# Long convolutions by quarters of the channels, two quarters one stage apart, and z kept unscaled

## The chip, the cores and the metric

One core of one Trainium2 chip runs the whole block in one launch. The metric is device microseconds per execution. Before the change three runs took 1247.49, 1248.54 and 1249.72 us (median 1248.54). The profiled execution that all rows come from took 1252.21 us.

## The reference, cut to what matters

A hybrid layer on x of 2048 positions by 1024 channels, all in float32:

```python
h = rms_norm(x, pre_g);  p = h @ w_in                       # 1024 -> 3072
hy = short_conv(p[:, :1536], conv_w, conv_b)                # 3 taps
v, gates = hy[:, :512], (hy[:, 512:1024], hy[:, 1024:])
k_f = two_sided_spectrum(hyena_filters(...))                # an MLP over positions
y = v
for o in range(2):
    y = gates[o] * fft_conv(y, k_f[:, o], hyena_d[o])       # two long convolutions
y_h = rms_norm(y * silu(z_h), norm_h_g)
y_p = rms_norm(multiscale_pool(u_p) * silu(z_p), norm_p_g)
out = x + rms_norm(concat(y_h, y_p) @ w_out, post_g)
```

## The kernel before, in words

The kernel is written in a tile framework. A planner takes the instructions in the order of the program as priorities, and gives each engine a fixed order in which an instruction may pass earlier ones that are not ready; each engine and each DMA queue then works in that order. Tiles of one tag share `bufs` buffers, and a new tile waits for the last use of the tile whose buffer it takes. PSUM has eight banks.

**Projection (0 to 600 us).** TensorE multiplies x by the columns of `w_in`, with every float32 operand split into two float32r parts (high and low) and three matmuls per product (`mm`, lines 313 to 320, five PSUM banks; `nm`, lines 541 to 543). x enters unnormalised; the rows' factors (`rb`, from `stat_x`) are multiplied in when a block leaves PSUM. In the first round, for each of four position blocks, `mm_tr` makes the pool branch's z and u. A z block is held in PSUM (`zps`) until the next round, when `stat_x` has its factors and `silu_evac` (line 325) reads it. The u blocks stay in PSUM too, up to `pool_means`.

**Long convolutions (600 to 1118 us).** Each is a transform of length 2048 written as matmuls in two steps, for 256 channels at a time: half `hf`, order `o`. The units run in the order (0,0), (1,0), (0,1), (1,1) as (order, half):

- `pre_k` makes the filter: `gen` (line 631, weights `HT`, 256 moving columns) makes filter values, DVE multiplies by the decay, GpSimd and DVE make sums and differences `sd`, `s1k` (line 644) does the first transform step, and the result goes to `BK`. `trans` then transposes 32x32 blocks on DVE.
- `pre_s` loads v and does the first transform step (`s`, three float32r matmuls in `mm3`) into `BS`.
- `gloop` is the loop over 16 groups: `kern` makes the filter's spectrum (`pk`), ACT copies it, two DMAs swap its halves (`kk`); `mult` makes the signal's spectrum (`px`) and the complex product with DVE, GpSimd and ACT; `back` is the inverse step (`pc`), which DVE copies into `BS`.
- `post0` finishes the inverse (`dd`, `py`), multiplies by the gate and does the first step of the next order into `BS`. `post1` does the last step of order 1, times the second gate, and stores `y_d`.
- `fill` computes the pool branch's half of the output product (`fp`, lines 769 to 771): 32 blocks that depend on nothing here. They are written between the stages.

There is one `BK` and one `BS` buffer of 32 KB per partition each. The banks are: `k` 2, `x` 2, `pk` 2, `c` 1, `f` 1; `s` shares `x`, and `py` uses `c` and `pk`.

**Output (1118 us to the end).** For four position blocks `split_y` makes the operand from `y_d` (first half of the channels) and from two `post1` of the second half; `out_mm` makes `po`; `finish` adds the stored `fp` part, normalises, adds x and stores.

All loads and stores of the convolutions are issued on SP's queue.

Of the kernel before, what the change touches and what calls it, by code (L numbers as in the profile page):

```python
# [37 lines left out]
def _tables():  # L38
# [53 lines left out]
    dt = dt.reshape(128, 8, 2, 2, 2, 256).transpose(4, 1, 0, 2, 3, 5)  # L92
# [13 lines left out]
def _layouts(inp):  # L106
# [33 lines left out]
    o["fwo"] = a["filt_w_out"][0].reshape(64, 2, 2, 2, 256)  # L140
# [8 lines left out]
def build(tc, I, out, debug=None):  # L149
# [442 lines left out]
    BK = kp.tile([P, R, 256, 2], F32, tag="BK", name="BK")  # L592
    BS = kp.tile([P, R, 256, 2], F32, name="BS")
# [8 lines left out]
    def trans(B, cbs=range(8)):  # L602
        for cb in cbs:
            ap = B[:, :, cb * 32:cb * 32 + 32].rearrange("p a c i -> p c a i")
            V.transpose(out=ap, in_=ap)  # L605

    def pre_k(o, hf):
        u = f"{o}{hf}"
        kw = wp.tile([P, 1024], F32, tag="wraw", name=f"kw{u}", bufs=1)
        wr, hd = kw[:, 0:512], kw[0:1, 512:768]  # L610
        for h in range(2):
            Q.dma_start(out=wr[64 * h:64 * h + 64].rearrange("p (a c) -> p a c", a=2), in_=I["fwo"][:, o, :, hf])
        Q.dma_start(out=hd, in_=I["hd"][o:o + 1, hf * 256:hf * 256 + 256])
        wh = hp.tile([P, 512], F32R, tag="kwh", name=f"kwh{u}", bufs=1)
        wl = hp.tile([P, 512], F32R, tag="kwl", name=f"kwl{u}", bufs=1)
        S.copy(out=wh, in_=wr)
        V.tensor_tensor(out=wl, in0=wr, in1=wh, op=ALU.subtract)
        sds = {}

        def gen(m):  # L620
            dc = kp.tile([P, 2, 2, 256], F32, tag="dec", name=f"dec{u}_{m}", bufs=2)
            (S if u == "00" and m < 2 else Q).dma_start(out=dc, in_=I["t_dec"][hf, m])
            ab = abp.tile([P, 2, 2, 256], F32, tag="ab", name=f"ab{u}_{m}", bufs=2)
            for i in range(2):
                n2 = 2 * m + i
                ps = psB.tile([P, 2, 256], F32, tag="k", name=f"gen{u}_{n2}", bufs=2)
                for dr in range(2):
                    c0 = n2 if dr == 0 else 16 - n2
                    lh = HT[:, c0 % R, c0 // R:c0 // R + 128]
                    for k_, wt in enumerate((wh, wl)):  # L630
                        T.matmul(ps[:, dr], lh, wt[:, dr * 256:dr * 256 + 256], start=(k_ == 0), stop=(k_ == 1))
                V.tensor_tensor(out=ab[:, i], in0=ps, in1=dc[:, i], op=ALU.mult)  # L632
                if n2 == 0:
                    G.tensor_tensor(out=ab[0:1, 0, 0], in0=ab[0:1, 0, 0], in1=hd, op=ALU.add)
            sd = wp.tile([P, 2, 2, 256], F32, tag="wh", name=f"sd{u}_{m}", bufs=3)
            G.tensor_tensor(out=sd[:, 0], in0=ab[:, :, 0], in1=ab[:, :, 1], op=ALU.add)  # L636
            V.tensor_tensor(out=sd[:, 1], in0=ab[:, :, 0], in1=ab[:, :, 1], op=ALU.subtract)
            sds[m] = sd

        def s1k(m):  # L640
            sd = sds.pop(m)
            for ri in range(2):
                ps = psB.tile([P, 2, 256], F32, tag="k", name=f"s1k{u}_{m}_{ri}", bufs=2)
                T.matmul(ps, f1[:, ri], sd[:, ri], start=True, stop=True)  # L644
                (V.tensor_copy if ri else S.copy)(out=BK[:, ri * 8 + m].rearrange("p c i -> p i c"), in_=ps)

        for m in range(9):
            if m < 8:
                gen(m)
# [12 lines left out]
    def pre_s(o, hf, cs=(0, 1)):
        for c in cs:
            for m in range(8):
                ut = abp.tile([P, 2, 2, P], F32R, tag="ut", name=f"ut{o}{hf}_{m}_{c}", bufs=3)
                Q.dma_start(out=ut.bitcast(F32), in_=v_d[hf, m, c])
                s1(f"{o}{hf}", m, c, ut)
            trans(BS, range(4 * c, 4 * c + 4))

    def gloop(o, hf, after=None):  # L670
        u = f"{o}{hf}"

        gs = [2 * (m // 2) + 16 * (m % 2) for m in range(16)]
# [13 lines left out]
        def mult(m):  # L687
            kk = kks.pop(m)
            px = psB.tile([P, 2, 256], F32, tag="x", name=f"px{u}_{m}", bufs=2)
            for i in range(2):  # L690
                T.matmul(px[:, i], gf[:, gs[m] + i], BS[:, gs[m] // 2, :, i], start=True, stop=True)  # L691
            xs = fp.tile([P, 2, 256], F32, tag="xs", name=f"xs{u}_{m}", bufs=2)
            S.mul(out=xs[0:64], in_=px[64:128], mul=-1.0)
            S.copy(out=xs[64:128], in_=px[0:64])  # L694
            yt = fp.tile([P, 2, 256], F32, tag="yt", name=f"yt{u}_{m}", bufs=3)
# [22 lines left out]
        back(15)  # L718
        trans(BS)

    def post0(hf):
        for c in range(2):
            cs = slice(128 * c, 128 * c + 128)
            uts = {}
            for m in range(9):
                if m < 8:
                    if m % 2 == 0:
                        gt = fp.tile([P, 4, P], F32, tag="gt", name=f"gt0{hf}_{m}_{c}", bufs=2)
                        Q.dma_start(out=gt, in_=g0_d[hf][:, 2 * m:2 * m + 4, cs])
                    dd = wp.tile([P, 2, 2, 2, P], F32R, tag="wl", name=f"dd{hf}_{m}_{c}", bufs=3)  # L730
                    src = BS.rearrange("p (r a) c i -> p r a c i", r=2)[:, :, m, cs].rearrange("p r c i -> p r i c")
                    S.copy(out=dd[:, 0], in_=src)
                    (V if m % 2 else G).tensor_tensor(out=dd[:, 1], in0=src, in1=dd[:, 0], op=ALU.subtract)
                    ps = psB.tile([P, 2, P], F32, tag=("c", "pk")[m % 2], name=f"py0{hf}_{m}_{c}", bufs=1 + m % 2)
                    for ri in range(2):
                        mm3(ps, 2 + ri, dd[:, 0, ri], dd[:, 1, ri], ri == 0, ri == 1)
                    g_ = gt[:, 2 * (m % 2):2 * (m % 2) + 2]
                    V.tensor_tensor(out=g_, in0=ps, in1=g_, op=ALU.mult)
                    ut = abp.tile([P, 2, 2, P], F32R, tag="ut", name=f"ut1{hf}_{m}_{c}", bufs=3)
                    S.copy(out=ut[:, 0], in_=g_)  # L740
                    V.tensor_tensor(out=ut[:, 1], in0=g_, in1=ut[:, 0], op=ALU.subtract)
# [205 lines left out]
```

## Time and profile before

| | us |
|---|---|
| median of three runs | 1248.54 |
| profiled execution / its span | 1252.21 / 1250.4 |
| PE busy | 1156.9 (93%) |
| DVE / POOL / ACT busy | 859.8 / 469.5 / 440.6 |
| projection, convolutions, output | 0 to 600, 600 to 1118, 1118 to 1250.4 |

A row of the view by line gives the line, the engine, the operation, the written and the read tiles, the shapes, the count, busy time and mean duration in ns, then the engine's idle time just before and what ended it. PE is a matmul, PEld the load of its weights. A float32 matmul appears as two recorded matmuls, a float32r matmul as one; both show as f32.

### The profile page before, as it was taken

Reading aid. Unit: us, or ns where it says so; the run is one execution under the profiler, and the core shown is the slowest. Engines: PE = TensorE matmul, PEld = TensorE weight load, DVE = VectorE, ACT = ScalarE, POOL = GpSimd, SP = SyncE. Lnnn points to the kernel's source line nnn. Section 1 sums busy time; section 2 is a strip of 40 time slices with the busy share of each in tenths; the row PEclk is TensorE's granted clock in tenths of the full one; section 3 lists DMA queues with packets and bytes.
Section 4 is the critical chain, followed back from the end, with each engine's and each line's share of the span. In section 5 each row is a group of like instructions: output and inputs, shape, how many; then the busy total and the mean of one; then the engine's idle time right before and its main releaser. Section 6 shows DMA issues by size and latency. Waiting matters only on the chain.

```text
span 1250.4 us, 16966 instructions
## 1 busy us (share of the span) xinstructions
PE 1156.9 (93%) x6040; PEld 945.9 (76%) x6040; DVE 859.8 (69%) x1419; ACT 440.6 (35%) x724; POOL 469.5 (38%) x416
## 2 busy tenths in 40 slices
PE   7799999999999999989888999999999999988894
PEld 5688888877887999889656686678677767777683
DVE  6965357446365576586688888685858974769887
ACT  7612111112111110210147563653375625833321
POOL 2302020413554296585515432430233421444444
PEclk9999999999999999999999999999999999999997
DMA  7204130421432353522786336546673367564764
GB/s 259 87 31 131 43 101 23 129 96 43 138 124 65 115 150 93 150 79 95 251 251 192 97 111 209 149 104 219 215 199 93 121 202 241 118 187 149 247 214 147
DMA packets 110628, 177.25 MB, mean 142 GB/s; under 512 B 11076, under 2 KB 58960, under 8 KB 109264
## 3 DMA queue, kind: packets, MB, share of 16 engines
q1 hardware_dynamic: 108720, 173.20, 45.0%
q10 hardware_dynamic: 1648, 2.44, 0.7%
q8 instruction: 48, 0.79, 0.3%
q0 software_dynamic: 176, 0.53, 0.1%
q14 instruction: 36, 0.29, 0.1%
HBM read 113.75 MB, written 44.56 MB: 127 GB/s over the span
## 4 chain that ended last, share of the span: by engine, by line
PE 54%; DVE 18%; DMA 10%; issue 8%; ACT 5%; POOL 5%; SPq 1%; DVEq 0%; POOLq 0%; ACTq 0%
PE mm L317 7%; PE mm L319 7%; PE mm L318 7%; PE pc L705 3%; PE pk L679 3%; PE s1k L644 3%; PE nm L541 3%; PE nm L542 3%; PE nm L543 3%; PE px L691 3%; DMA a2p<-a 2%; PE fp L769 2%; PE fp L770 2%; PE fp L771 2%; DVE o L899 2%
## 5 line engine op out<-in xcount | busy, mean ns | idle before, releaser
L541 PE MATMUL nm<-wh,XH 128*128 128x256 f32 x512 | 144.8, 283 | 7.5 <-DVE a L548 6.7
L542 PE MATMUL nm<-wl,XH 128*128 128x256 f32 x512 | 144.8, 283 | 0.0
L543 PE MATMUL nm<-wh,XL 128*128 128x256 f32 x512 | 144.7, 283 | 0.0
L697 POOL TENSOR_TENSOR xs<-xs,kk 128x512 f32<-128x512 f32 x64 | 84.8, 1329 | 119.1 <-ACT xs L694 79.7
L548 DVE SCALAR_TENSOR_TENSOR a<-nm,r_nat,wc 128x256 f32<-128x256 f32 x192 | 81.5, 475 | 51.4 <-DMA a0p<-a 13.6
L541 PEld LDWEIGHTS nm<-wh,XH 128*128 128x128 f32 x512 | 97.5, 190 | 8.6 <-DVE a L548 7.8
L317 PE MATMUL mm<-XH,wh 128*128 128x512 f32 x256 | 103.0, 402 | 0.0
L319 PE MATMUL mm<-XH,wl 128*128 128x512 f32 x256 | 102.2, 399 | 0.0
L318 PE MATMUL mm<-XL,wh 128*128 128x512 f32 x256 | 101.5, 396 | 0.0
L636 POOL TENSOR_TENSOR sd<-ab 128x512 f32<-128x512 f32 x32 | 53.0, 1655 | 118.8 <-DVE ab L632 118.4
L543 PEld LDWEIGHTS nm<-wh,XL 128*128 128x128 f32 x512 | 96.9, 189 | 0.0
L542 PEld LDWEIGHTS nm<-wl,XH 128*128 128x128 f32 x512 | 96.7, 189 | 0.0
L705 PE MATMUL pc<-yt,gi 128*128 128x256 f32 x256 | 69.1, 392 | 14.7 <-DVE BS L706 7.8
L605 DVE STREAM_TRANSPOSE BS<-BS 128x1024 f32<-128x1024 f32 x64 | 73.5, 1209 | 7.4 <-ACT BS L660 7.4
L696 DVE TENSOR_TENSOR yt<-px,kk 128x512 f32<-128x512 f32 x64 | 44.0, 687 | 44.5 <-ACT xs L694 24.5
L691 PE MATMUL px<-BS,gf 128*128 128x256 f32 x256 | 69.9, 394 | 2.8 <-DVE BS L605 1.8
L679 PE MATMUL pk<-BK,gf 128*128 128x256 f32 x256 | 71.9, 393 | 0.2
L705 PEld LDWEIGHTS pc<-yt,gi 128*128 128x128 f32 x256 | 44.5, 189 | 34.7 <-DVE BS L706 15.8
L660 ACT COPY BS<-s 128x512 f32<-128x512 f32 x64 | 39.8, 628 | 79.8 <-PE s L589 76.0
L644 PE MATMUL s1k<-sd,f 128*128 128x512 f32 x128 | 63.5, 605 | 4.7 <-POOL sd L636 3.9
L698 DVE TENSOR_TENSOR yt<-yt,xs 128x512 f32<-128x512 f32 x64 | 54.0, 844 | 14.0 <-POOL xs L697 11.9
L317 PE MATMUL mm<-XH,whz 128*128 128x512 f32 x128 | 54.1, 423 | 9.7 <-ACT XH L284 6.1
(208 smaller groups left out, 3089.4 us busy)
## 6 DMA issues: line engine op xcount, KB each, us to landing
kk<-kk SPq DMA_DIRECT2D x128, 128.0 KB
fy<-yp_d SPq DMA_DIRECT2D x32, 512.0 KB
dec<-t_dec SPq DMA_DIRECT2D x30, 512.0 KB
wr<-w SPq DMA_DIRECT2D x16, 512.0 KB
ut<-v_d SPq DMA_DIRECT2D x32, 256.0 KB
gt<-g_d SPq DMA_DIRECT2D x32, 256.0 KB
op_d<-fo SPq DMA_DIRECT2D x32, 256.0 KB
o<-op_d SPq DMA_DIRECT2D x32, 256.0 KB
```

Of the source, the lines that this page charges most:

```text
L317: T.matmul(ps, wh, XH[lb][:, d], start=(d == 0), stop=False)
L318: T.matmul(ps, wh, XL[lb][:, d], start=False, stop=False)
L319: T.matmul(ps, wl, XH[lb][:, d], start=False, stop=(d == NT - 1))
L541: T.matmul(ps, xh[:, d, ls], wh, start=(d == 0), stop=False)
L542: T.matmul(ps, xh[:, d, ls], wl, start=False, stop=False)
L543: T.matmul(ps, xl[:, d, ls], wh, start=False, stop=(d == NT - 1))
L548: V.scalar_tensor_tensor(out=a[s], in0=ps, scalar=r_nat[:, l2:l2 + 1], in1=wc[:, s], op0=ALU.mult, op1=ALU.mult)
L644: T.matmul(ps, f1[:, ri], sd[:, ri], start=True, stop=True)
L679: T.matmul(pk[:, i], gf[:, gs[m] + i], BK[:, gs[m] // 2, :, i], start=True, stop=True)
L691: T.matmul(px[:, i], gf[:, gs[m] + i], BS[:, gs[m] // 2, :, i], start=True, stop=True)
L697: G.tensor_tensor(out=xs, in0=xs, in1=kk[:, 1], op=ALU.mult)
L705: ins = T.matmul(pc[:, i], gi[:, gs[m] + i], yt[:, i], start=True, stop=True)
```

## The change: what it does

The convolutions run in quarters of 128 channels. `BK` and `BS` become two buffers of 16 KB each. `pre_k`, `pre_s`, `gloop`, `post0` and `post1` no longer emit their work; each returns a list of steps. `run` merges the lists: the main list (mostly a loop) in order, the steps of each side list at even places up to 0.88 of the main one. The loop has 8 groups of four 128-column matmuls instead of 16 groups of two 256-column ones. `pc` is copied by ACT instead of DVE; all of `dd`'s subtracts are on GpSimd. The banks are `k` 2, `s` 2 (for `s` and `py`), `pk` 1, `x` 1, `c` 1, `f` 1. The result of the third quarter is stored and loaded again too, so that the output stage holds one `py1` per block. `xt` has two buffers instead of three. In the first round the first three z blocks are copied out of PSUM unscaled, and scaled later from SBUF.

```diff
+    def raw_evac(ci, lb, ps):
+        z = st.tile([P, 512], F32, tag="z", name=f"z{ci}_{lb}", bufs=3)
+        S.copy(out=z, in_=ps)
+        return z
...
         zn = mm_tr(0, 1, lb)
+        if lb < 3:
+            zn = raw_evac(0, lb, zn)
...
-            zs.append(silu_evac(0, lb - 1, zps))
+            zs.append(silu_evac(0, lb - 1, zps, zps))
...
+    def run(main, *sides, upto=0.88):
+        ev = [(i / len(main), 0, i, f) for i, f in enumerate(main)]
+        for k, sd in enumerate(sides):
+            ev += [((j + 0.5) / len(sd) * upto, k + 1, j, f) for j, f in enumerate(sd)]
+        for e in sorted(ev, key=lambda e: e[:3]):
+            e[3]()
...
-            ab = abp.tile([P, 2, 2, 256], F32, tag="ab", name=f"ab{u}_{m}", bufs=2)
-            for i in range(2):
-                n2 = 2 * m + i
-                ps = psB.tile([P, 2, 256], F32, tag="k", name=f"gen{u}_{n2}", bufs=2)
...
-                        T.matmul(ps[:, dr], lh, wt[:, dr * 256:dr * 256 + 256], start=(k_ == 0), stop=(k_ == 1))
+            ab = abp.tile([P, 4, 2, P], F32, tag="ab", name=f"ab{u}_{j}", bufs=2)
+            for h in range(2):
+                ps = psB.tile([P, 2, 2, P], F32, tag="k", name=f"gen{u}_{j}_{h}", bufs=2)
+                for i in range(2):
...
+                            T.matmul(ps[:, i, dr], lh, wt[:, dr * P:dr * P + P], start=(k_ == 0), stop=(k_ == 1))
...
-            pk = psB.tile([P, 2, 256], F32, tag="pk", name=f"pk{u}_{m}", bufs=2)
-            for i in range(2):
-                T.matmul(pk[:, i], gf[:, gs[m] + i], BK[:, gs[m] // 2, :, i], start=True, stop=True)
-            kk = wp.tile([P, 2, 2, 256], F32, tag="wl", name=f"kk{u}_{m}", bufs=3)
+            pk = psB.tile([P, 4, P], F32, tag="pk", name=f"pk{u}_{m}", bufs=1)
+            for k in range(4):
+                T.matmul(pk[:, k], gf[:, 4 * m + k], BK[o, q][:, 2 * m + k // 2, :, k % 2], start=True, stop=True)
+            kk = wp.tile([P, 2, 4, P], F32, tag="kk", name=f"kk{u}_{m}", bufs=2)
...
-            V.tensor_copy(out=BS[:, gs[m] // 2].rearrange("p c i -> p i c"), in_=pc)
+            S.copy(out=BS[q][:, 2 * m:2 * m + 2].rearrange("p a c i -> p a i c"), in_=pc)
...
-        kern(0)
-        kern(1)
-        for m in range(16):
-            mult(m)
-            if m + 2 < 16:
-                kern(m + 2)
+        r = [lambda: kern(0)]
+        for m in range(8):
+            if m + 1 < 8:
+                r.append(lambda m=m: kern(m + 1))
+            r.append(lambda m=m: mult(m))
             if m:
-                back(m - 1)
...
-    pre_k(*units[0])
...
-    gloop(0, 0)
-    post0(0)
-    pre_k(1, 0)
-    fill(range(0, 8))
-    gloop(1, 0)
...
+    run(pre_k(0, 0) + [tables], pre_s(0), fills(0, 5), upto=1.0)
+    run(gloop(0, 0), seq(pre_k(0, 1), pre_s(1)), fills(5, 9))
+    run(gloop(0, 1), post0(0), pre_k(1, 0), fills(9, 12))
+    run(gloop(1, 0), post0(1), pre_k(1, 1), fills(12, 15))
+    run(gloop(1, 1), seq(post1(0), pre_s(2)), pre_k(0, 2), fills(15, 18))
+    run(gloop(0, 2), seq(post1(1), pre_s(3)), pre_k(0, 3), fills(18, 21))
+    run(gloop(0, 3), post0(2), pre_k(1, 2), fills(21, 24))
+    run(gloop(1, 2), post0(3), pre_k(1, 3), fills(24, 28))
...
+    run(gloop(1, 3, held), post1(2),
+        [lambda ct=ct: split_wo(op, ct, 0, O0[:, 0, ct], O0[:, 1, ct], "wor") for ct in range(4)])
+    for cb in range(4):
+        trans(BS[3], cb)
```

`held` issues the last four fills behind the last `pc`, as before.

## Rows read from the trace of the kernel before

**Rows 1.** The page's first section: busy us (share of the span) xinstructions.
```profile
PE 1156.9 (93%) x6040; PEld 945.9 (76%) x6040; DVE 859.8 (69%) x1419; ACT 440.6 (35%) x724; POOL 469.5 (38%) x416
```

**Rows 2.** Busy time by stretch: length, then each engine, clock, DMA share, GB/s.
```profile
600.00:1118.00 518.00, 474.23 (x2302) 359.52 (x2300) 392.46 (x529) 274.07 (x469) 177.44 (x128) 0.99 0.58 172
675.00:700.00 25.00, 24.30 (x106) 19.45 (x107) 20.66 (x31) 21.05 (x37) 11.99 (x9) 1.00 0.56 135
716.00:752.00 36.00, 34.30 (x229) 29.54 (x228) 31.70 (x54) 25.18 (x50) 12.51 (x9) 1.00 0.38 120
800.00:825.00 25.00, 25.00 (x109) 19.84 (x109) 17.43 (x27) 19.77 (x35) 10.99 (x9) 0.99 0.48 111
1055.00:1080.00 25.00, 23.24 (x101) 17.90 (x100) 17.85 (x27) 21.49 (x37) 9.55 (x8) 1.00 0.66 176
1118.00:1250.40 132.40, 105.90 (x506) 87.56 (x504) 109.38 (x276) 37.96 (x86) 57.02 (x30) 0.91 0.57 192
0.00:100.00 100.00, 86.30 (x378) 68.72 (x379) 70.81 (x139) 50.06 (x62) 23.25 (x23) 0.95 0.38 129
```

**Rows 3.** Waits of PE from 600 to 1118: us in total, times, longest.
```profile
PE pc L705 <- DVE BS L706: 7.8, 9, 2.2
PE pc L705 <- DVE yt L698: 6.6, 5, 1.9
PE s L587 <- DMA ut<-v_d: 4.3, 6, 1.4
PE fp L769 <- ACT fo L793: 3.9, 6, 0.8
PE s1k L644 <- POOL sd L636: 3.9, 5, 1.5
PE fp L769 <- DMA fy<-yp_d: 3.1, 2, 2.2
```

**Rows 4.** Waits of PE from 0 to 100 us.
```profile
PE mm L317 <- DVE r4t L195: 3.6, 1, 3.6
```

**Rows 5.** Waits of PE from 1118 us to the end.
```profile
PE py L755 <- DVE rp L186: 5.4, 1, 5.4
PE py L755 <- DVE gt L757: 2.3, 1, 2.3
```

**Rows 6.** PE in order of time: start, length, instruction, count.
```profile
29.94 1.95 PE L260 MATMUL wp<-pw,wu 128*128 128x128 f32 x16
31.72 0.95 PE L300 MATMUL ssx<-one,xsq 128*128 128x1 f32 x8
...
629.54 0.28 PE L631 MATMUL gen<-kwl,HT 128*128 128x256 f32 x1
629.65 0.28 PE L631 MATMUL gen<-kwh,HT 128*128 128x256 f32 x1
...
676.27 1.07 PE L691 MATMUL px<-BS,gf 128*128 128x256 f32 x4
...
843.76 0.40 PE L755 MATMUL py<-f,BS 128*128 128x128 f32 x2
844.00 0.40 PE L756 MATMUL py<-f,BS 128*128 128x128 f32 x2
```

**Rows 7.** The view by line, shapes apart (columns as above).
```profile
L631 PE MATMUL gen<-kwh,HT 128*128 128x256 f32 x128 | 37.8, 318 | 3.0 <-DVE a L548 1.5 <-DVE BK L645 1.5
L706 DVE COPY BS<-pc 128x512 f32<-128x512 f32 x64 | 43.8, 684 | 4.6 <-PE pc L705 4.5
L660 ACT COPY BS<-s 128x512 f32<-128x512 f32 x64 | 39.8, 628 | 79.8 <-PE s L589 76.0 <-PE py L756 2.9
L693 ACT ACTIVATE xs<-px 64x512 f32<-64x512 f32 x64 | 37.9, 593 | 19.4 <-ACT kk L682 8.8 <-issue 4.9 <-PE px L691 2.4
L733 POOL TENSOR_TENSOR dd<-BS,dd 128x512 fp32r<-128x512 f32 x16 | 22.5, 1413 | 36.6 <-ACT dd L732 32.9 <-DVE gt L738 3.8
L733 DVE TENSOR_TENSOR dd<-BS,dd 128x512 fp32r<-128x512 f32 x16 | 12.8, 798 | 0.7 <-ACT dd L732 0.6
```

More of the change, by code (lines that the diff above doesn't have):

```diff
@@ L636, in gen, with s1k @@
             G.tensor_tensor(out=sd[:, 0], in0=ab[:, :, 0], in1=ab[:, :, 1], op=ALU.add)
             V.tensor_tensor(out=sd[:, 1], in0=ab[:, :, 0], in1=ab[:, :, 1], op=ALU.subtract)
-            sds[m] = sd
-        def s1k(m):
-            sd = sds.pop(m)
+            sds[j] = sd
+        def s1k(j):
+            sd = sds.pop(j)
             for ri in range(2):
-                ps = psB.tile([P, 2, 256], F32, tag="k", name=f"s1k{u}_{m}_{ri}", bufs=2)
-                T.matmul(ps, f1[:, ri], sd[:, ri], start=True, stop=True)
-                (V.tensor_copy if ri else S.copy)(out=BK[:, ri * 8 + m].rearrange("p c i -> p i c"), in_=ps)
@@ L662, in pre_s @@
[L662 to L673, printed above, removed]
+                ps = psB.tile([P, 2, 2, P], F32, tag="k", name=f"s1k{u}_{j}_{ri}", bufs=2)
@@ new lines, in s1k @@
+                T.matmul(ps.rearrange("p a i c -> p (a i c)"), f1[:, ri], sd[:, ri], start=True, stop=True)
+                dst = BK[o, q][:, ri * 8 + 2 * j:ri * 8 + 2 * j + 2].rearrange("p a c i -> p a i c")
+                (V.tensor_copy if ri else S.copy)(out=dst, in_=ps)
+        r = [weights]
+        for j in range(5):
+            if j < 4:
+                r.append(lambda j=j: gen(j))
+            if j:
+                r.append(lambda j=j: s1k(j - 1))
+        return r + [lambda cb=cb: trans(BK[o, q], cb) for cb in range(4)]
@@ new lines, in rows, with s1, pre_s, step @@
+    def rows(q):
+        return BS[q].rearrange("p (r a) c i -> p r a c i", r=2)
+    def s1(q, u, m, src):
+        pss = psB.tile([P, 2, 2, P], F32, tag="s", name=f"s1_{u}{q}_{m}", bufs=2)
+        for ri in range(2):
+            mm3(pss[:, ri], ri, src[:, 0], src[:, 1])
+        S.copy(out=rows(q)[:, :, m].rearrange("p r c i -> p r i c"), in_=pss)
+    def pre_s(q):
+        def step(m):
+            if m == 0:
+                new_s(q)
+            ut = abp.tile([P, 2, 2, P], F32R, tag="ut", name=f"ut{q}_{m}", bufs=3)
+            Q.dma_start(out=ut.bitcast(F32), in_=v_d[q // 2, m, q % 2])
+            s1(q, "0", m, ut)
+        return [lambda m=m: step(m) for m in range(8)] + [lambda cb=cb: trans(BS[q], cb) for cb in range(4)]
@@ L702, in back @@
             yt = yts.pop(m)
-            pc = psB.tile([P, 2, 256], F32, tag="c", name=f"pc{u}_{m}", bufs=1)
-            for i in range(2):
-                ins = T.matmul(pc[:, i], gi[:, gs[m] + i], yt[:, i], start=True, stop=True)
-            V.tensor_copy(out=BS[:, gs[m] // 2].rearrange("p c i -> p i c"), in_=pc)
+            pc = psB.tile([P, 2, 2, P], F32, tag="c", name=f"pc{u}_{m}", bufs=1)
+            for k in range(4):
+                ins = T.matmul(pc[:, k // 2, k % 2], gi[:, 4 * m + k], yt[:, k], start=True, stop=True)
@@ L707, in back @@
+            S.copy(out=BS[q][:, 2 * m:2 * m + 2].rearrange("p a c i -> p a i c"), in_=pc)
             if after:
                 after(m, ins)
-        kern(0)
-        kern(1)
-        for m in range(16):
-            mult(m)
-            if m + 2 < 16:
-                kern(m + 2)
-            if m:
-                back(m - 1)
[L718 to L741, printed above, removed]
-                    uts[m] = ut
-                if m:
-                    s1(f"1{hf}", m - 1, c, uts.pop(m - 1))
-            trans(BS, range(4 * c, 4 * c + 4))
@@ L747, in post1 @@
-    def post1(hf, lb, cb):
-        ct = hf * 2 + cb
-        gt = fp.tile([P, 512], F32, tag="gt", name=f"gt1{hf}_{lb}{cb}", bufs=2)
-        Q.dma_start(out=gt, in_=g1_d[ct][:, lb * 512:lb * 512 + 512])
-        ps = psB.tile([P, 4, P], F32, tag="c" if hf else "pk", name=f"py1{hf}_{lb}{cb}", bufs=1 if hf else 2)
+        r = [lambda: kern(0)]
[3 more added lines that the diff above has]
+            r.append(lambda m=m: mult(m))
+            if m:
+                r.append(lambda m=m: back(m - 1))
@@ new lines, in gloop, with post0, step @@
+        r.append(lambda: back(7))
+        return r
+    def post0(q):
+        uts, gts = {}, {}
+        def step(m):
+            if m < 8:
+                if m % 2 == 0:
+                    gts[m // 2] = fp.tile([P, 4, P], F32, tag="gt", name=f"gt0{q}_{m}", bufs=2)
+                    Q.dma_start(out=gts[m // 2], in_=g0_d[q // 2][:, 2 * m:2 * m + 4, (q % 2) * P:(q % 2) * P + P])
+                dd = wp.tile([P, 2, 2, 2, P], F32R, tag="dd", name=f"dd{q}_{m}", bufs=2)
+                src = rows(q)[:, :, m].rearrange("p r c i -> p r i c")
+                S.copy(out=dd[:, 0], in_=src)
+                G.tensor_tensor(out=dd[:, 1], in0=src, in1=dd[:, 0], op=ALU.subtract)
+                ps = psB.tile([P, 2, P], F32, tag="s", name=f"py0{q}_{m}", bufs=2)
+                for ri in range(2):
+                    mm3(ps, 2 + ri, dd[:, 0, ri], dd[:, 1, ri], ri == 0, ri == 1)
+                g_ = gts[m // 2][:, 2 * (m % 2):2 * (m % 2) + 2]
+                V.tensor_tensor(out=g_, in0=ps, in1=g_, op=ALU.mult)
+                ut = abp.tile([P, 2, 2, P], F32R, tag="ut", name=f"ut1{q}_{m}", bufs=3)
+                S.copy(out=ut[:, 0], in_=g_)
+                V.tensor_tensor(out=ut[:, 1], in0=g_, in1=ut[:, 0], op=ALU.subtract)
+                uts[m] = ut
+            if m:
+                s1(q, "1", m - 1, uts.pop(m - 1))
+        return ([lambda cb=cb: trans(BS[q], cb) for cb in range(4)] + [lambda m=m: step(m) for m in range(9)]
+                + [lambda cb=cb: trans(BS[q], cb) for cb in range(4)])
@@ L757, in post1, with step @@
         V.tensor_tensor(out=gt, in0=ps, in1=gt, op=ALU.mult)
         return gt
+    def post1(q):
+        def step(lb):
+            Q.dma_start(out=y_d[q][:, lb * 512:lb * 512 + 512], in_=py1(q, lb))
+        return [lambda cb=cb: trans(BS[q], cb) for cb in range(4)] + [lambda lb=lb: step(lb) for lb in range(4)]
     def split_wo(pl, ct, dh, hi, lo, tag):
@@ L812, in build, with fill @@
-    pre_s(0, 1)
-    pre_k(0, 1)
-    fill(range(8, 16))
-    gloop(0, 1)
-    post0(1)
-    pre_k(1, 1)
-    fill(range(16, 28))
+    def fill(k, late=None):
+        dh, l2 = divmod(k, R)
+        fh, fl = fill_w(dh)
+        yt = (abp if late else ff).tile([P, 2, 4, P], F32R, tag="ab" if late else "yf", name=f"fy{k}", bufs=2)
+        Q.dma_start(out=yt.bitcast(F32), in_=yp_d[l2])
+        ps = psB.tile([P, 512], F32, tag="f", name=f"fp{k}", bufs=1)
+        mm_out(ps, yt[:, 0], yt[:, 1], fh, fl)
+        ot = (late or ff).tile([P, 512], F32, tag="wor" if late else "fo", name=f"fo{k}", bufs=2)
+        S.activation(out=ot, in_=ps, func=AF.Copy, scale=rpn[:, l2:l2 + 1])
+        Q.dma_start(out=op_d[dh, l2], in_=ot)
@@ new lines, in fills, with tables @@
+    def fills(a, b):
+        return [lambda k=k: fill(k) for k in range(a, b)]
+    def tables():
+        for t_, n_ in ((gf, "t_gf"), (gi, "t_gi")):
+            for a in range(0, 32, 8):
+                Q.dma_start(out=t_[:, a:a + 8], in_=I[n_][:, a:a + 8])
+    run(pre_k(0, 0) + [tables], pre_s(0), fills(0, 5), upto=1.0)
+    run(gloop(0, 0), seq(pre_k(0, 1), pre_s(1)), fills(5, 9))
+    run(gloop(0, 1), post0(0), pre_k(1, 0), fills(9, 12))
+    run(gloop(1, 0), post0(1), pre_k(1, 1), fills(12, 15))
@@ L858, in split_y @@
         G.tensor_tensor(out=ya[:, 0], in0=ya[:, 0], in1=ya[:, 1], op=ALU.add)
-        for cb in range(2):
-            gt = post1(1, lb, cb)
-            S.copy(out=yb[:, 0, 2 + cb], in_=gt)
-            V.tensor_tensor(out=yb[:, 1, 2 + cb], in0=gt, in1=yb[:, 0, 2 + cb], op=ALU.subtract)
+        for cb in (2, 3):
+            if cb == 2:
+                gt = fp.tile([P, 512], F32, tag="yt", name=f"yc{lb}", bufs=3)
+                Q.dma_start(out=gt, in_=y_d[2][:, ls])
+            else:
+                gt = py1(3, lb)
+            S.copy(out=yb[:, 0, cb], in_=gt)
+            V.tensor_tensor(out=yb[:, 1, cb], in0=gt, in1=yb[:, 0, cb], op=ALU.subtract)
             S.activation(out=gt, in_=gt, func=AF.Square)
@@ L884, in out_mm @@
             yield i, (r[i, 0], r[i, 1])
+    xv = I["x"].rearrange("(a b) d -> a b d", b=R)
+    ov = out.rearrange("(a b) d -> a b d", b=R)
     def finish(lb, rr, i, pss):
         l2 = 4 * lb + i
[L888 removed]
+        xt = wp.tile([P, D], F32, tag="kk", name=f"xt{l2}", bufs=2)
         Q.dma_start(out=xt, in_=xv[:, l2])
```

158 lines of the change are left out of this document (72 added, 86 removed).

## The prediction

> **What bounds the kernel now.** I read the page's first two sections first [rows 1]: TensorE is busy 1156.9 of 1250.4 us and DVE only 859.8, so whatever lengthens TensorE's own stream lengthens the kernel unless it fills time in which TensorE waits. Then busy time by stretch [rows 2]. The convolutions run from 600 to 1118 us; TensorE is busy for 474.2 of those 518 us and idle for 43.8. In one stretch of them, 800 to 825, it never idles; from 675 to 700 it idles 0.7 us, from 1055 to 1080 1.8. So the matmul queue can be kept nearly full, but is not always. In the second step of the first convolution (716 to 752) VectorE is busy 31.7 of 36 us: locally the second limit. The output stretch has VectorE at 109.4 of 132.4. Third, who ended TensorE's waits in the convolutions [rows 3]: the biggest are `pc` waiting for its one PSUM bank (DVE's copy out, 7.8) or for its input (6.6), then the load of `ut` (4.3), `fp` behind its one bank (3.9), `s1k` behind GpSimd's `sd` (3.9). They are many and short: what is missing is other work to put there. Last, single waits at both ends [rows 4, 5].
>
> A matmul's mean duration is no price here, because matmuls overlap. What counts is the spacing of starts in a dense row, (length of the row − one matmul) / (count − 1) [rows 6]: single-pass f32r with 256 columns 0.115 to 0.12 us (629.54, 629.65); f32 with 256 columns (1.07 − 0.39)/3 = 0.227; f32 with 128 columns (1.95 − 0.27)/15 = 0.112 (`wp`), and 0.118 where an operand is strided (`py`: two each from 843.76 and from 844.00, 0.237 apart). A row of one-column matmuls, each with new weights, still takes (0.95 − 0.16)/7 = 0.113 (`ssx`): there the weight load is the price.
>
> **The change, part by part.** All sums are against the profiled execution, 1252.2 us (span 1250.4 and 1.8 around it); it lies 3.7 above the median of the runs, and I take 3.7 off at the end.
>
> *Filter generation by quarters.* `gen` now multiplies 128 columns per matmul instead of 256, so 256 matmuls [rows 7] become 512, each with its own weight load. Before: 256 × 0.118 = 30.2 us. After: no f32r matmul below 256 columns is in the trace. Were it only streaming, 0.059 × 512 = 30.2, no change; at the weight load's pace 0.113 × 512 = 57.9, +27; if it ran as slowly as an f32 pair of 128 columns, 0.236 × 512 = 121, +91. I take +27, since `ssx` and `wp` show that new weights do not come faster than 0.112.
> The Trainium skill (TensorE: Matmul & The Clock Gate, Back-to-back issue gap) gives a sustained 81 ns per matmul of 128 columns with its weight load. By that figure the 512 would take an estimated 41.5 us, +11 instead of +27. No row here is as close as 81 ns, and `ssx` and `wp` contradict it for 4-byte weights.
>
> *pk, px, pc by quarters.* Four units of 16 steps, two matmuls and two records each, are 256 records per tile kind; each becomes two of 128 columns: 768 × 0.227 = 174 us before, 1536 × 0.112 = 172 to 1536 × 0.118 = 181 after. Bounds −2 and +7; I take +2.
> `s1k` (512 columns), `s`, `py`, `fp`, `po` keep shape and number.
>
> *Two quarters one stage apart.* BK and BS become two buffers each. A loop no longer runs alone: beside the loop of one quarter stand the post stage of the quarter before it, the next filter and three or four fills, dealt out evenly. TensorE's idle 43.8 us [rows 2] is what this can take. Bounds: none stays (as in 800 to 825), or 518/25 × 1.8 = 37 stays (as in 1055 to 1080); I take the rate of 675 to 700, 0.7 per 25, so 14.5 stays: −29. Going by waits [rows 3]: `pc` has four other streams to stand behind, fills no longer queue on their own bank, `s1k` comes with other matmuls after `gen`; the first waits after 600 and part of the `ut` loads stay. Late next is the post stage's `s` behind DVE's `ut`, since DVE is the second limit in that stage (716 to 752). I add −4 for the weight loads that wait with the matmul and go out late (bounds 0 and −15).
>
> *What moves between engines.* The copy of `pc` goes from DVE (64 × 0.684 = 43.8 us) to ACT, at the price of a same-size copy there, 64 × 0.628 = 40 [rows 7]. The half of the `dd` subtracts on DVE (16 × 0.798 = 12.8) goes to GpSimd (16 × 1.413 = 22.6). In the convolutions that leaves DVE 392 − 57 = 335, ACT 274 + 40 = 314, GpSimd 177 + 23 = 200, of some 510 us: hidden beside TensorE, cost 0 [rows 2]. If that cover goes, the price is a place in ACT's queue (first rival). Transposes: still 96.
>
> *PSUM.* `pk` and `px` fall to one bank, `s` and `py` get two of their own. The cycle of `px`'s bank is 0.93 of matmuls, two ACT halves of some 0.593, one DVE read like that of `pc` (0.684) [rows 7], about 3.4 us with hand-overs, and a step now comes about every 7 us (510 us by 72 steps, the first stage counted as one loop): hidden, 0. In the last loop, with few others beside it, 8 × (3.4 − 2.8) = 5 us may show; that is inside the 14.5.
>
> *SP's queue.* Twelve small loads more (weights and skip term per quarter), four stores and four loads of 256 KB for the third quarter's result; in it stand the `kk` swaps (still 128), now with `fy`, `dec`, `ut` and `gt` loads between them. A load behind a swap that waits for ACT is late by one step; buffers in front of it are two or three. Cost 0; without that cover it is the `fy` and `ut` waits, 3.1 and 4.3 [rows 3], inside the 37. The `tables` loads are written behind the first filter.
>
> *z unscaled.* The first three z blocks are copied out of PSUM at once instead of being held until their row statistics are known: three copies of 0.63 on ACT, which is busy 50 of the first 100 us, so hidden. It removes the 3.6 us wait at 57 us [rows 4], and with it part of the half-clock time: the granted clock of the first 100 us averages 0.95 [rows 2], 10 us at 1.2 GHz, which cost 5. Bounds 0 (if the x block is as late) and −3.6 − 5 = −8.6; I take −5, the wait and some of the rest.
>
> *Output.* `py` now comes once per block, not twice, with two banks. Its waits, 5.4 and 2.3 us [rows 5], should go; with VectorE at 109 of 132 some of it comes back as a wait for it. Bounds 0 and −9; I take −6. `xt` has two buffers instead of three; 16 steps share the 132 us, so a load still has one step, some 8 us, ahead of its use: 0.
>
> Sum: +27 + 2 − 29 − 4 − 5 − 6 = −15: 1237 in a profiled execution, 1233.5 beside the median; rounded to 1234.
>
> **Rivals.**
> *ScalarE's queue takes over (slower).* The copy that frees `pc`'s single bank stands on ACT, in order with `kk`, `xs`, `s`, `dd`, `ut`. If in half of the 64 steps it stands behind one pair of half copies (2 × 0.593, as L693 in [rows 7]) while TensorE's next matmul is `pc`, that is 38 us: −15 + 38 = +23, 1271. Break-even is 13 steps. For: ACT is already at 21 of 25 us inside a loop [rows 2], and what DVE gives up is all put there. Against: over a stage it is at 314/510.
> *No better cover.* The planner already mixes `gen`, `s1k` and `fp` into the loops, so the written mix changes little; idle stays at 43.8, the 33 us come back: +18, 1266. For: `pc` and `gen` lie side by side in the trace already. Against: one BK and one BS forbid most of it today, and the waits of [rows 3] name next steps that had nothing else beside them.
> *They cancel.* Idle falls to about 29: within 0.2% of 1248.5.
> *Weights hide.* The 128-column `gen` streams at 0.06: −27 more, 1207. Against: `ssx`. The Trainium skill's 81 ns lies between this and my forecast, and belongs to this rival.
>
> **How the numbers follow.** Forecast 42%, with its own range 1222 to 1246 (idle 5 to 25). ScalarE's queue 20%, no better cover 14%, cancel 12%, weights hide 12%. A measurement here tells about 0.2%, 2.5 us: faster 0.42 + 0.12 = 0.54, same 0.12, slower 0.34. The range for 8 in 10 goes from 1213 (part of the hidden weights) to 1272 (the slow rivals' prices). The +91 of a slow 128-column f32r is left outside, since `ssx` shows one load as the bound.
>
> **What would show it.** `gen` spaced 0.113: step right; 0.06 or 0.24: wrong. TensorE idle of 15 us in the convolutions, most of it in the first and last stage: right; 30 or more, with `pc` waiting for an ACT copy: the first rival. The wait near 57 us and both `py` waits gone. Wrong altogether if TensorE's idle falls as said and the time still rises: then the added matmul time was sized too low.

## The result: slower, and where the time went

The changed kernel takes 1266.49 us (1265.75 to 1268.70) against 1249.13, a ratio of 1.0132 with a 95% interval of 1.011 to 1.0154: some 17 us slower, less than 2%, where 1234 was forecast. Its profiled execution has a span of 1264.0 us, 13.6 more than before.

First section of the page after, against [rows 1]:
```profile
PE 1174.8 (93%) x7064; PEld 1012.7 (80%) x7064; DVE 823.8 (65%) x1343; ACT 480.5 (38%) x795; POOL 488.4 (39%) x436
```
Busy time by stretch after, against [rows 2]: length, PE, PEld, DVE, ACT, POOL, clock, DMA share, GB/s. The convolutions now run from 597 to 1138 us, the output stretch from there:
```profile
0.00:100.00 100.00, 89.38 (x410) 71.38 (x411) 74.19 (x142) 52.32 (x67) 24.41 (x25) 0.97 0.41 137
597.00:660.00 63.00, 53.99 (x296) 42.41 (x296) 33.20 (x45) 20.93 (x34) 17.29 (x16) 0.92 0.80 275
597.00:1138.00 541.00, 499.65 (x3384) 434.54 (x3384) 357.25 (x459) 318.33 (x546) 199.22 (x149) 0.98 0.57 170
1138.00:1264.00 126.00, 97.26 (x426) 78.04 (x424) 106.21 (x267) 32.81 (x78) 53.85 (x27) 0.90 0.57 192
```
The same stretch of before, cut at its first and last matmul, and its first 60 us:
```profile
602.00:1118.00 516.00, 472.23 (x2285) 357.52 (x2283) 391.19 (x525) 274.07 (x469) 176.52 (x127) 0.99 0.58 171
600.00:660.00 60.00, 49.59 (x256) 34.82 (x255) 45.37 (x61) 20.02 (x34) 21.16 (x18) 1.00 0.76 248
```
The convolutions take 541 us instead of 516 (+25); they begin 5 us earlier (597, not 602); the output takes 126.0 instead of 132.4 (−6.4). 25 − 5 − 6.4 = 13.6. TensorE's idle time in the convolutions is 541 − 499.65 = 41.3 us, before 43.8: the idle that was to fill is still there. The granted clock is an average over time at 2.4 and at 1.2 GHz. In the first 63 us of the convolutions it is 0.92, where the kernel before has 1.00: an estimated 63 × 0.08 = 5 us less of TensorE's clock, for which the prediction has no term. No run here tests what they cost.

Waits of PE after, from 597 to 1138 us, against [rows 3] (us in total, times, longest):
```profile
PE pc L746 <- DVE yt L739: 9.1, 17, 2.2
PE px L732 <- DVE yt L737: 5.2, 16, 1.1
PE py L601 <- POOL dd L772: 3.5, 4, 0.9
PE fp L815 <- issue: 2.9, 1, 2.9
PE s1k L682 <- DVE ab L670: 2.8, 3, 2.4
```
`pc`'s wait for the copy that frees its bank (7.8) is gone, and no wait of PE for the new copy on ACT stands in its place. What grew is the wait for `yt`, the product of the loop step (`pc` 6.6 to 9.1, `px` 0.8 to 5.2).

PE, ACT, DVE and POOL of after in order of time, in the last steps of the second quarter's loop (some lines left out; start, length, engine, line, instruction, count, idle before):
```profile
762.18 1.07 PE L720 MATMUL pk<-BK,gf 128*128 128x128 f32 x8
...
763.01 0.31 PE L669 MATMUL gen<-kwh,HT 128*128 128x128 f32 x1
...
763.10 1.28 POOL L738 TENSOR_TENSOR xs<-xs,kk 128x512 f32<-128x512 f32 x1 [4.00 <-ACT xs L735]
763.15 0.28 PE L669 MATMUL gen<-kwl,HT 128*128 128x128 f32 x1
...
763.26 0.27 PE L669 MATMUL gen<-kwh,HT 128*128 128x128 f32 x1
...
764.41 0.58 ACT L722 COPY kk<-pk 64x512 f32<-64x512 f32 x1 [0.72 <-POOL xs L738]
764.41 0.69 DVE L739 TENSOR_TENSOR yt<-yt,xs 128x512 f32<-128x512 f32 x1 [0.67 <-POOL xs L738]
765.01 0.58 ACT L723 COPY kk<-pk 64x512 f32<-64x512 f32 x1
...
765.25 1.13 PE L746 MATMUL pc<-yt,gi 128*128 128x128 f32 x8 [0.28 <-DVE yt L739]
765.62 0.59 ACT L734 ACTIVATE xs<-px 64x512 f32<-64x512 f32 x1
...
766.22 0.58 ACT L735 COPY xs<-px 64x512 f32<-64x512 f32 x1
...
766.88 1.27 POOL L738 TENSOR_TENSOR xs<-xs,kk 128x512 f32<-128x512 f32 x1 [2.50 <-ACT xs L735]
```
Two things are read here. `gen` starts are 0.11 apart (763.15, 763.26), as forecast, and `pk` (1.07 − 0.28)/7 = 0.113. And here a loop step is a ring: GpSimd's product (1.28) frees a `kk` buffer, ACT writes two `kk` and two `xs` halves (4 × 0.59), the next product follows at once, 3.78 us after the last. TensorE's own three groups of the step are 8 × 0.113 each, 2.7 us, so other work must fill 1.1 us of such a step. Only one pair of products in most stages, and several around the last loop, stand that close; the others are 4 to 16 us apart.

By tile, `py` (first fence) and `pc` (second), then all instructions (third), around and behind the seam between two stages of after (length, PE, PEld, then DVE or ACT, in the third all engines; clock, DMA share, GB/s). In the 26 us at the seam five groups of `pc` run and no `py`. Four of the five close the old loop (the last starts at 769.0), one opens the new one. The old post stage is done at 753; the next one needs the last `pc` copied and `BS` transposed, and its first `py` starts at 779.5.
```profile
753.00:779.00 26.00, 0.00 (x0) 0.00 (x0) 0.39 (x1) 1.00 0.41 101
779.00:814.00 35.00, 8.00 (x48) 6.30 (x48) 2.92 (x7) 1.00 0.51 156
```
```profile
753.00:779.00 26.00, 5.46 (x40) 4.85 (x40) 2.51 (x4) 1.00 0.41 101
779.00:814.00 35.00, 3.22 (x25) 3.07 (x24) 2.53 (x4) 1.00 0.51 156
```
```profile
753.00:779.00 26.00, 24.74 (x184) 22.73 (x183) 20.85 (x26) 17.36 (x30) 8.54 (x7) 1.00 0.41 101
779.00:814.00 35.00, 33.02 (x220) 27.60 (x220) 26.16 (x37) 23.27 (x43) 20.21 (x14) 1.00 0.51 156
```
TensorE's idle is 1.3 us of the 26 and 2.0 of the 35: the crowded part is no idler than the rest.

### The profile page after: what moved, and what is told of

Read it like the earlier page. It is cut to its first block, busy times and chain, and to the rows that moved or that the text cites. A ratio compares the mean times of both kernels' runs of the same rounds, so it can differ in the third digit from the quotient of the medians.

```text
span 1264.0 us, 19047 instructions
## 1 busy us (share of the span) xinstructions
PE 1174.8 (93%) x7064; PEld 1012.7 (80%) x7064; DVE 823.8 (65%) x1343; ACT 480.5 (38%) x795; POOL 488.4 (39%) x436
## 5 line engine op out<-in xcount | busy, mean ns | idle before, releaser
L738 POOL TENSOR_TENSOR xs<-xs,kk 128x512 f32<-128x512 f32 x64 | 82.2, 1284 | 217.7 <-ACT xs L735 202.0
L623 DVE STREAM_TRANSPOSE BS<-BS 128x1024 f32<-128x1024 f32 x64 | 76.5, 1221 | 14.0 <-ACT BS L747 14.0
L732 PE MATMUL px<-BS,gf 128*128 128x128 f32 x512 | 73.6, 281 | 5.2 <-DVE yt L737 5.2
L746 PE MATMUL pc<-yt,gi 128*128 128x128 f32 x512 | 69.4, 278 | 9.1 <-DVE yt L739 9.1
L746 PEld LDWEIGHTS pc<-yt,gi 128*128 128x128 f32 x512 | 63.4, 191 | 16.0 <-ACT kk L722 8.3
L732 PEld LDWEIGHTS px<-BS,gf 128*128 128x128 f32 x512 | 66.0, 190 | 12.1 <-DVE yt L737 7.7
L720 PE MATMUL pk<-BK,gf 128*128 128x128 f32 x512 | 69.3, 276 | 1.3 <-ACT kk L723 1.3
L720 PEld LDWEIGHTS pk<-BK,gf 128*128 128x128 f32 x512 | 64.3, 188 | 6.5 <-issue 4.3
```

Of the source, the lines that this page charges most:

```text
L720: T.matmul(pk[:, k], gf[:, 4 * m + k], BK[o, q][:, 2 * m + k // 2, :, k % 2], start=True, stop=True)
L732: T.matmul(px[:, k], gf[:, 4 * m + k], BS[q][:, 2 * m + k // 2, :, k % 2], start=True, stop=True)
L738: G.tensor_tensor(out=xs, in0=xs, in1=kk[:, 1], op=ALU.mult)
L746: ins = T.matmul(pc[:, k // 2, k % 2], gi[:, 4 * m + k], yt[:, k], start=True, stop=True)
```

## Experiments

Times are told as ratios to the kernel before in the same comparison; 0.01 is 12.5 us, and a difference of two ratios is uncertain by some 4 to 6 us. Except where the order is kept, the planner lays out the order of all engines anew after each edit. Five edits that were to help or to do nothing (a second `px` bank, fills moved, the copy back on VectorE, swaps on ScalarE's queue, a third `kk` buffer) came out 4 to 8 us slower than the changed kernel, so a difference of that size between two kernels with different orders need not be the edit's own, and a gain of a few us can be hidden by one.

**The matmul time of `gen`.** First in the kernel before, each `gen` matmul split into two of 128 columns:
```
+ for c_ in range(2): T.matmul(ps[:, dr, c_*P:c_*P+P], lh, wt[:, dr*256+c_*P : dr*256+c_*P+P], ...)
```


> The kernel before with each 256-column gen matmul written as two of 128 columns (512 weight loads instead of 256), nothing else. Theory A (TensorE's stream is the bound, weight loads at 0.112 us each are paid in full): gen spaced 0.112, +27 us, 1276; up to 8 less if some falls into idle. Theory B (other engines pace the stages, TensorE has slack): under +10.


1298.0 us, 1.0384 (1.0354 to 1.0413): +47, more than either theory. Its convolutions (row further down) take 561 us instead of 516: TensorE's busy time grew by 37 and its idle by 8. Some 27 of the 37 are the added matmuls; an estimated 561 × 0.02 = 11 go with the granted clock, 0.97 instead of 0.99. Then the opposite, in the changed kernel: only the high parts are multiplied.
```
- for k_, wt in enumerate(st_["w"]):
+ for k_, wt in enumerate(st_["w"][:1]):
```


> The changed kernel without the low part of the filter weights in gen: 256 matmuls of 128 columns instead of 512 (the filter loses its low bits). Theory A: -27 to -30 us, 1238. Theory B (ScalarE's queue, single banks): -10 or less, TensorE's idle grows by what is taken out.


1.0037 (1.0019 to 1.0056), 12 us less than the changed kernel for 28 us of matmuls. Both leave the question whether the planner's new order did it. So, in either arrangement, low-part matmuls were taken out of the finished order (192 and 196 of 256), all else kept; like the run before, both leave part of the filters out:


> The changed kernel with 192 of the 256 low-part generator matmuls (kwl) taken out after the order had been set, so that every other instruction of every engine stands where it stood; this leaves out part of the long filters. 192 at the measured 0.112 us are 21.5 us of TensorE's stream. Theory A (TensorE's stream sets the time of the convolutions, so that each added weight load of the generator is paid in full): at least 17 us less than the changed kernel's 1266.5, so 1245 to 1249. Theory B (a stage is paced by the chain pk, kk, px, yt, pc through ScalarE and VectorE with a single bank for px): 5 to 11 us less, and the idle of TensorE between 597 and 1138 us grows from 41 to over 50 us. It also tells how far the run with only high parts, whose order was planned anew, was short of A because of its order.

> The kernel before with its generator matmuls split into two of 128 columns (1298.0 us), and 196 of the 256 low-part ones taken out after the order had been set; this leaves out part of the long filters. 196 at 0.112 us are 22 us of TensorE's stream. If TensorE's stream is the bound in the kernel before's arrangement: 1276 to 1280. If that arrangement too is paced off TensorE (the changed kernel gave back 3.6 of 21.5 us): 1290 to 1296, and then the 47 us of the split were mostly other work moved, not matmul time.


1.0131 (1.0105 to 1.0158): nothing of 21.5 us by the ratio, 4.8 by the spans. And 1.0365, 2 us less than the split kernel's 1.0384 (4.9 by the spans), for 22 us. By stretch, the kernel before with split matmuls; the changed kernel with high parts alone; and with fewer in the same order:
```profile
602.00:1163.00 561.00, 509.54 (x2541) 394.76 (x2542) 390.72 (x525) 274.15 (x469) 174.22 (x126) 0.97 0.54 158
```
```profile
599.00:1131.00 532.00, 482.40 (x3132) 414.81 (x3130) 366.26 (x458) 318.88 (x545) 198.00 (x149) 0.97 0.58 173
```
```profile
597.00:1133.00 536.00, 485.31 (x3202) 416.82 (x3201) 358.37 (x460) 318.18 (x546) 200.93 (x150) 0.97 0.57 172
```
TensorE's idle in the last two is 49.6 and 50.7 us, where the full kernel has 41.3. So of the 21.5 us taken out in the kept order 9.4 became idle and 5 came off the stretch (536 us, not 541). The rest agrees with what the clock took back: of seven pieces into which 597 to 1140 us was cut, three were granted less than in the changed kernel, an estimated 6.8 us in all. The piece with the largest difference, in the changed kernel and with fewer in the same order:
```profile
1000.00:1080.00 80.00, 74.85 (x525) 66.21 (x524) 61.53 (x76) 53.50 (x93) 35.04 (x25) 1.00 0.54 157
```
```profile
1000.00:1080.00 80.00, 72.69 (x478) 62.50 (x477) 56.64 (x71) 52.69 (x91) 36.32 (x27) 0.96 0.54 159
```
Even with these 6.8 added the gain would be 12 at most, not the 17 that theory A asked for. TensorE, 92% busy, does not by itself set the time of the convolutions, in the changed kernel or in the split one; the kernel before as it stood was not tested so. Theory A falls.

**Z and the output alone.** The kernel before with z unscaled, and then with a second bank for `py` in the output too:


> The kernel before with the first three z blocks copied out of PSUM unscaled, nothing else. The ramp in the changed kernel ended 5 us earlier, so -5 us (1244) if that is all there is; 0 if the following stages wait for something else.

> The kernel before with z unscaled and with a second bank for py in the output stage, and nothing else of the change. z was worth 4 us alone. If the output stage's two waits for py (7.7 us) were on the path: 1239 to 1244. If they come back as waits for VectorE's o, as in the changed kernel: 1245 to 1248.


0.9969 (0.9954 to 0.9984), −4 us, where −5 was expected: the fastest kernel here that computes everything. With the `py` bank 1.0018 (0.9999 to 1.0037): no gain, and 6 us more than z alone. Its waits of PE from 1115 us:
```profile
PE po L774 <- DVE o L904: 10.9, 2, 8.4
PE po L775 <- DVE O L770: 1.9, 2, 1.2
```
The waits for `py`, 7.7 us in [rows 5], came back behind VectorE's `o`.

**The written mix.** The changed kernel with a loop written whole and then the side lists whole; and with the sides spread over a whole loop instead of 0.88 of it:
```
- for e in sorted(ev, key=lambda e: e[:3]):
+ for e in sorted(ev, key=lambda e: e[1:3]):
```
```
- def run(main, *sides, upto=0.88):
+ def run(main, *sides, upto=1.0):
```


> The changed kernel with run() writing the main list first and then each side list whole, so that only the planner mixes. If the written mix is what covers waits: +15 to +40 us, TensorE's idle in the convolutions up from 41. If the planner mixes as well by itself (no better cover): within 5 us of 1266.

> The changed kernel with the side lists spread over the whole of a loop instead of its first 88 percent; no work is added or left out. If the written mix sets the pace by when a stage's post and filter work are done (the next loop's transposes then come later): 5 to 15 us slower. If TensorE's stream did: within 3 us of 1266.5. An even spread that takes the thin last steps of a stage as cover: 3 to 8 us faster.


Unmixed 1.0823, 86 us slower than the changed kernel. Spread evenly 1.0021 (1.0001 to 1.0041): 14 us faster than the changed kernel by one number that adds and removes no work, more than the 3 to 8 expected at best, and nearly level with before. Its convolutions, and PE's waits in them:
```profile
597.00:1127.00 530.00, 499.60 (x3384) 439.59 (x3384) 354.92 (x459) 316.69 (x546) 202.44 (x150) 0.97 0.59 174
```
```profile
PE pk L720 <- ACT kk L723: 5.8, 9, 1.3
PE px L732 <- DVE yt L737: 4.4, 7, 1.1
PE pc L746 <- DVE yt L739: 3.8, 2, 2.2
```
The same 3384 matmul records in 530 us instead of 541; idle 30.4 instead of 41.3; `pc`'s waits for `yt` 3.8 us in 2 places instead of 9.1 in 17. Two things keep this from being a proof that the loop's crowding cost the time. Of the 11 us less idle 4.7 lie between 600 and 660 us (PE busy 57.2 against 52.5), in the first stage, whose spread was 1.0 already and whose order only came out new; they brought no time, at a granted clock of 0.86 instead of 0.91. And the seam is nearly as it was. Around it, all instructions and then `pc` alone, with five groups and again no `py`:
```profile
753.00:778.00 25.00, 23.20 (x177) 21.64 (x176) 22.52 (x29) 16.46 (x29) 9.87 (x8) 1.00 0.49 116
```
```profile
753.00:778.00 25.00, 5.32 (x40) 4.87 (x40) 3.02 (x5) 1.00 0.49 116
```
Idle there is 1.8 us, more than the 1.3 without the edit; over the six seams TensorE's waits in these last loop steps add up to 6.0 us instead of 7.9. From the first product of the first loop to that of the last it takes 423 us instead of 433; 4.5 and 4.0 us of the ten lie in two of the seven stages between (second and sixth).

**Single suspects off TensorE.** A second bank for `px` (`bufs=2`, `fp` and `yss` on `s`); the first stage without fills (`fills(0, 9)` beside the second); the `pc` copy back on VectorE (`S.copy` to `V.tensor_copy`):


> The changed kernel with two PSUM banks for px (the filter's fp and the sums yss share the two banks of s instead). B: waits of px for yt (5.2 us on TensorE and 7.7 us on its weight loads) go and the time falls by 6 to 12 us, to 1255 to 1260. A: the waits go but are replaced by others, within 3 us of 1266.5; fp and s1 sharing a tag may cost up to 4 us more.

> The changed kernel with none of the five filter fills beside the first stage of the convolutions; all nine stand beside the second. Theory C (the first stage loses some 10 us to fills that wait for their loads at the head of TensorE's queue, and to the half clock behind them): the stretch 597 to 660 us is 6 to 12 us shorter and the time 1255 to 1261. A and B: the stretch gets shorter only by the work that left it (5 fills of six 512-column matmuls), the second stage longer by as much, and the time stays within 3 us of 1266.5.

> The changed kernel with the copy of pc back on VectorE. If the copy on ScalarE delays kk for the other quarter (the rival in which ScalarE's queue takes over) the time falls by 4 to 10 us. A: no change within 3 us. B: VectorE is 76% busy beside the loops and yt gets later still, so 3 to 10 us slower.


1.0186, 1.0186 and 1.0195 (each ± 0.004): none helps. With the second bank the waits of `px` for `yt` went (0.5 left) and others came; without fills the first stage ran at a granted clock of 0.81, 597 to 660, instead of 0.92.

Then `kk`: sharing four buffers with `dd`; its swaps issued by GpSimd (`G.dma_start`) or ScalarE (`S.dma_start`); a third buffer of its own:


> The changed kernel with kk and dd sharing four buffers of one tag instead of two each (the kernel before let them share three). Theory D (a loop step is paced by kk: ScalarE's next copy waits for GpSimd to have read the buffer two steps back, 13.5 us of waits between 753 and 1002 us, and behind that copy stand xs, ut, dd and BS): ScalarE's waits for POOL xs go and the time falls by 6 to 14 us, 1252 to 1260. Theory A (TensorE's stream): within 3 us of 1266.5. It may get 2 to 4 us slower if dd comes to wait for kk.

> The changed kernel with the 128 kk swaps issued by GpSimd instead of SP. Theory E (loads stand behind swaps in SP's queue, whose head waits for ScalarE's copy 58.6 us between 753 and 1002 us; kw, dec, wo and ut then come late and ScalarE's and VectorE's queues stop on them): waits for kw, dec, wo and ut go and the time falls by 5 to 12 us, unless GpSimd's own issues, some 1 us each and 128 of them, slow its products (then 5 to 20 us slower, with POOL busy up by 100 us). Theory A: within 3 us.

> The same with the 128 swaps issued by ScalarE, right behind the copies they wait for. E: loads no longer stand behind the swaps, and the time falls by 5 to 12 us, less what 128 issues of some 0.05 to 0.6 us cost on ScalarE (6 to 77 us, spread over eight loops in which it is the pacing engine). If the issues are dear, it is slower than 1266.5 by 10 or more, and the swaps were rightly on SP. Theory A: within 3 us.

> The changed kernel with a third buffer for kk (the one that held the filter's weights, which get a tile of their own; in the last loop kk has two as before). Theory D (a loop step is paced by kk's two buffers): ScalarE's waits for POOL xs, 13.5 us between 753 and 1002 us, go, and the time falls by 6 to 12 us, to 1254 to 1260. Theory F (the step's chain itself, copies, product, sum and bank, paces it, however many buffers stand in front): the waits go and pc's and px's waits for yt stay; within 3 us of 1266.5.


1.0343, 1.0245, 1.0195 and 1.0168 (1.0131 to 1.0205). Three fences follow. The first, of the shared buffers, shows the wait that sharing made, `py` behind `dd`. The second is ACT from 753 to 1002 us in the changed kernel, the third the same with a third buffer, where ACT's wait for GpSimd's product no longer stands:
```profile
PE py L601 <- POOL dd L772: 15.1, 20, 0.9
```
```profile
ACT fo L838 <- PE fp L817: 21.5, 12, 3.5
ACT kk L722 <- POOL xs L738: 13.5, 12, 1.9
```
```profile
ACT fo L841 <- PE fp L820: 25.7, 12, 3.4
ACT BS L750 <- PE pc L749: 19.0, 19, 3.9
ACT kwh L652 <- DMA kw<-fwo: 11.1, 2, 6.5
```
ACT then waits for TensorE and for loads instead. The two products that stood 3.8 us apart in a stage now stand 3.2 apart, and the time does not fall: theory D, the ring through `kk`, is not borne out. Nor is E: moved to GpSimd the swaps cost that engine time of its own, and on ScalarE's queue they brought nothing.

**Work taken from the other engines.** GpSimd's product on 128 of 512 columns; each transpose on 8 of 32 channels; then both together with the high parts alone. All three leave part of the result out:
```
+ G.tensor_tensor(out=xs[:, 0], in0=xs[:, 0], in1=kk[:, 1, 0], op=ALU.mult)
+ ap = B[:, :, cb * 32:cb * 32 + 8].rearrange("p a c i -> p c a i")
```


> The changed kernel with GpSimd's product in each loop step on 128 of 512 columns (three quarters of xs stay unmultiplied: part of the complex product is left out). F: a step's chain loses some 0.9 of 3.8 us; over five dense steps in each of eight loops that is 36 us at the most, and 10 to 20 us of it show: 1246 to 1256. D: about the same, since the kk buffer comes free 0.9 us earlier. Theory A (TensorE's stream) and theory G (the stage is paced by the post stage's chain py, gt, ut, s and by VectorE): within 4 us of 1266.5.

> The changed kernel with each transpose on 8 instead of 32 channel columns (three quarters of BS and BK stay untransposed: part of the data movement is left out). It takes some 58 of VectorE's 77 us of transposes away, most of them in front of yt and at the ends of stages. G: VectorE is the hidden pace of a stage, so 12 to 25 us less, 1242 to 1254. F and D: 2 to 6 us less. A: within 3 us.

> The changed kernel with only the high-part generator matmuls, GpSimd's product on 128 of 512 columns, and the transposes on a quarter of the columns (all three leave part of the computation out). One path: the gains of 11, 8 and 9 us add, some 1238 (1234 to 1243). Parallel paths of nearly equal length, each capping the gain of the others' removal: more than the sum, below 1232, since shortening all of them lifts the caps. If something not touched (ScalarE, loads, the post stage's hand-overs) paces the stages: no better than the best of the three, 1250 to 1257.


1.0096 (1.0062 to 1.0131), 1.0074 (1.0045 to 1.0102) and 0.9887 (0.9851 to 0.9922): 4.5, 7 and 31 us less than the changed kernel. The parts give 12 + 4.5 + 7 = 24 alone and 31 together, within the uncertainty the sum or more. (The transposes lost 79 us of VectorE's time, of 114.5; the expectation had counted those of `BS` alone.) The 4.5 and 7 are no larger than what a new order does, the 31 are. They fit work on TensorE, GpSimd and VectorE lying by turns on the path that sets a stage, with none of them the bound by itself; that is argued, not shown.

## Why the prediction was wrong, by its own steps

- *Two quarters one stage apart* (−29, and −4 for weight loads) is the step that failed. Idle was to fall from 43.8 to 14.5 and is 41.3. Counted in work, the convolutions got 27 of `gen` and 8.3 of `py` from the output, 35 us, and grew by 25: some 10 us were covered, not 33. I took the rate of one good stretch of 25 us of the kernel before for the whole, and took TensorE's idle for something that more streams fill. What the runs show instead: TensorE keeps waiting on hand-overs from other engines. With its matmuls taken out in a kept order, 9.4 of 21.5 us turned into more idle and at most 5 into time; another spread of the same work gave 14 us; less work on three engines together gave 31. The sides are not "dealt out evenly" either: the 26 us at the seam shown have no `py`. But they are no idler than the rest, a shorter ring brought nothing, and the better spread left the seam nearly as it was: that the crowding costs the time is not shown.
- *Filter generation* (+27) was right as TensorE's time and wrong as the kernel's: 28 us out gave 12, and 21.5 out in a kept order 0 to 5, with up to 7 more lost again to the lower clock. The sentence at its root failed too: that whatever lengthens TensorE's stream lengthens the kernel unless it fills its waits. I read 93% busy as the bound.
- *pk, px, pc by quarters* (+2): 0.113 apart, 1536 × 0.113 = 173.6 against 174 before: 0, inside the bounds.
- *The copy of `pc` on ACT* (0), *PSUM* (0), *SP's queue* (0): right as far as undoing each did not help. VectorE's busy time in the convolutions fell to 357 us, not to the 335 I had, and loop steps do not come every 7 us: some are 3.8 apart, others 12. `kk` fell from three shared buffers to two; I did not price it, and a third one brings nothing.
- *z unscaled* (−5): right. `mm`'s wait of 3.6 [rows 4] is gone, the convolutions begin 5 us earlier, and alone it gives 4.
- *Output* (−6): the right number for the wrong reason. In the output stretch `py` has 32 matmul records instead of 102; 70 × 0.118 = 8.3 us moved into the convolutions. The waits came back, as in the kernel before with two banks; PE after, from 1138 us:
```profile
PE po L815 <- DVE o L946: 8.9, 3, 5.9
PE po L816 <- DVE O L811: 1.2, 1, 1.2
```
- The rival *No better cover* gave 1266 and idle 43.8, both close. Its reason fails, though: it said that the written mix changes little, and another written mix costs 86 us (none at all) or gives 14 (spread evenly). *ScalarE's queue takes over* fails: no wait for the copy, and no gain with it on VectorE.

Still open is which chain sets the 57 to 64 us of a stage, and by what the even spread helps. A run with the changed kernel's order and another spread can't exist, since the spread is the order; and no suspect taken alone gave more than 12 us.

## What to carry to other kernels

An engine that is busy 92% of a stretch is not therefore its bound: take some of its work out with the order kept, and see whether the time, the idle or the granted clock moves. A gain from cover is not to be extrapolated from the best stretch; ask which work is ready in each part of a stage, and try the spread of the mix before and beside a new tiling, since here one constant of it was worth 14 of the 17 us that the change cost. Of the change, unscaled z alone is worth keeping, 0.9969 of the time before.

## What the hardware showed that was not expected

An f32r matmul of 128 columns with new weights starts 0.11 us after the last, hardly sooner than one of 256 [rows 6]: half the columns save next to nothing. A swap issued from GpSimd's queue cost that engine 0.53 us: with 128 of them its busy time went from 488.4 to 555.9 us. And with matmuls taken out of a kept order the rest ran at a lower granted clock: 0.96 against 1.00 from 1000 to 1080 us.
